# Seven-product matmul of an MLP: pairing whole token blocks instead of token halves

## Chip, cores and metric

The kernel runs on one core of one Trainium2 chip. The metric is the device time of one execution in microseconds (us). The core's engines are TensorE (PE in the rows; PEld is its weight load), VectorE (DVE), ScalarE (ACT), GpSimd (POOL) and SyncE (SP), which issues the DMAs.

## The reference

One layer of a diffusion backbone works on 1152 tokens (1024 latent, 128 context) of 1024 features. Two mixers and their output projection come first; the change touches only the MLP behind them:

```
h   = RMSNorm_pre2(x) * (1 + scale2) + shift2
x   = x + gate2 * RMSNorm_post2(relu(h @ W1)^2 @ W2)     W1 1024 x 4096, W2 4096 x 1024
```

All is fp32. The kernel splits each operand into a high part (rounded to TensorE's fp32r format) and a low part (the rest), and a product is three matmuls: high x high, high x low, low x high.

## The kernel before

**Tokens and tiles.** The normalised tokens lie in SBUF feature-major, in three blocks of 384 tokens (`h2H[b]`, `h2L[b]`, 128 partitions x 8 chunks of 128 features x 384). A scheduler with its own costs (`Sched`) sets the order of all work up to this point; it ends with `Q.run()`, and the two early groups of the first column (L1980) are its last matmuls. From there on the order is the order in which the code is written.

**First product, plain columns.** The hidden features are 32 columns of 128, two to a pair, 16 pairs. The first two pairs (`NPL = 2`, columns m = 0 to 3) are computed plainly in `plain`: for each token block 8 chunks x 3 matmuls of 128x384 (L2050 to L2052), then ScalarE's Relu and Square, and one store of the column to `Fd` in DRAM. `w1_load` fetches a column of W1 (512 KB) into the one tile `raw`; `w1_split` makes w1H on ScalarE (L1718) and w1L on VectorE (L1719). Between the blocks `work` runs: `build` forms the token operands of the seven-product scheme.

**First product, the other 14 pairs.** `strassen` uses the Winograd form of the 2x2 scheme: A is a pair's weights (two columns by two halves of the features), B the tokens (two halves of the features by two halves of the tokens, 576 each, `HT`). Seven products of 4 chunks x 3 matmuls, each on two pieces of 288 columns (L2194), replace eight. A token half is not a block: `h_copies` gathers its parts by DMA into `B11`, and, for want of room, spills `B21` and `B22` to DRAM (`Hd`); they are read back (L2162) when the blocks' own tiles are given up. `T1` to `T4` are sums of these operands, made by `build`.

**Weights of a pair.** `w1_pair` loads both columns (L2102). `w_sums` makes three sums on VectorE (L2126 to L2128), `w_split` the high and low part of one of seven weight words (L2137 on ScalarE, L2138 on VectorE; S4 also needs L2135). They run as hooks between the steps of the pair ahead. Eight pairs also carry 16 small matmuls of the second gate (`late_mm`).

**Evacuation.** Products accumulate in PSUM banks called x, y and z; ScalarE copies x out three times (t1, u2, u4, L2200), VectorE adds them to y or z (L2205), squares (L2180), and the result goes to `Fd` (L2183).

**Second product.** `mlp2` runs 16 groups, each 9 token tiles x 2 halves x 6 matmuls of 128x512 (L2296 to L2298). `g_load` reads back one group's `Fd` and two rows of W2 (L2231, L2234), `g_w` and `g_f` split them (L2240, L2241, L2254, L2255). For the first group these are hooks of the last pair.

Of the kernel before, what the change touches and what calls it, by code (L numbers as in the profile page):

```python
# [10 lines left out]
F32 = mybir.dt.float32  # L11
# [7 lines left out]
D = 1024  # L19
# [183 lines left out]
def hymba_kernel(tc, a, o):  # L203
# [1764 lines left out]
    Q.add("A", ca(1024), lambda: w1_split(0), r=["w1l"], w=["w1s"], take=[w1w], prio=400)  # L1968
    nop("h2k", [("me", j, f) for j in range(6, 10) for f in range(4)])
# [31 lines left out]
    def operand(x, pool):
        HO[x] = [pool.tile([128, 4, HT], F32R, tag=f"o{x}{q}", name=f"o{x}{q}") for q in "HL"]
    for x in ("T1", "T2", "T3", "T4", "B11"):
        operand(x, tb)


    SEG = [((0, 0, 384, 0), (1, 0, 128, 384), (2, 256, 320, 512)), ((1, 128, 384, 0), (2, 0, 256, 256), (2, 320, 384, 512))]

    def h_copies(dst, half, kj, blocks):
        for b, c0, c1, d in SEG[half]:  # L2010
            if b in blocks:
                for q in range(2):
                    SY.dma_start(out=dst[q][:, :, d:d + c1 - c0].bitcast(F32),
                                 in_=(h2H, h2L)[q][b][:, 4 * kj:4 * kj + 4, c0:c1].bitcast(F32))

    def build(k):

        qA = bp.tile([128, 2, HT], F32, tag="q0", name="qA")
        qB = bp.tile([128, 2, HT], F32, tag="q1", name="qB")
        for t, half in ((qA, 0), (qB, 1)):  # L2020
            for b, c0, c1, d in SEG[half]:
                yield lambda t=t, b=b, c0=c0, c1=c1, d=d: V.tensor_tensor(
                    out=t[:, :, d:d + c1 - c0], in0=h2H[b][:, k::4, c0:c1].bitcast(F32), in1=h2L[b][:, k::4, c0:c1].bitcast(F32),
                    op=ALU.add)
# [17 lines left out]
    def plain(m, work):  # L2042

        wH, wL = w1q.pop(m)
        f = bp.tile([128, NT], F32, tag="pf", name="pf")
        f2 = f.rearrange("p (a c) -> p a c", a=2)
        for b in (1, 2, 0):
# [5 lines left out]
            r = bp.tile([128, BLK], F32, tag="r", name="r")  # L2053
            S.activation(out=r, in_=ps, func=AF.Relu)
# [362 lines left out]
```

## Time and profile before

| | |
|---|---|
| median of 3 runs | 1762.05 us (1756.42 to 1762.86) |
| profiled execution, its own time | 1766.09 us |
| its span, first to last instruction | 1764.3 us |
| TensorE busy | 1623.9 us (92%), 13731 matmuls |
| VectorE / ScalarE / GpSimd busy | 64% / 39% / 17% |
| mean granted TensorE clock | 0.968 of full |
| chain that ended last | TensorE 66%, VectorE 13%, DMA 7% |

The busy shares are means over stages with different limits, so the stages are read apart: plain columns to 1011.49 us, first pair to 1047.92, eight pairs with late matmuls to 1236.28, five without to 1347.62, then the second product. A matmul's own duration in the rows (0.29 to 0.40 us) overlaps with its neighbours'; the distance between two starts is what a matmul costs in a stream.

### The profile page before, as it was taken

The page shows a single profiled execution, that of the slowest core. Times are in us where ns is not written, and L with a number is a line of the kernel's source. Part 1 is how long each engine was busy: PE and PEld are TensorE (multiplying, and loading weights), DVE is VectorE, ACT ScalarE, POOL GpSimd, SP SyncE. Part 2 cuts the span into 40 slices and gives each one's busy share as a digit, 9 for nine tenths or more (in the row PEclk, how much of TensorE's full clock was granted, in tenths as well). Part 3 has the DMA queues.
Part 4 walks back from the last instruction along what each step waited for, and adds up shares of the span by engine and source line. Part 5 has one row for each costly group of instructions (what it writes and reads, how often), then busy time and mean ns, then how long its engine had stood idle before and what let it go on. Part 6 is the DMA issues. An engine that isn't in the chain of part 4 may idle for free.

```text
span 1764.3 us, 33783 instructions
## 1 busy us (share of the span) xinstructions
PE 1623.9 (92%) x13731; PEld 1372.9 (78%) x13731; DVE 1134.1 (64%) x1882; ACT 680.9 (39%) x1283; POOL 304.5 (17%) x425
## 2 busy tenths in 40 slices
PE   6799988898899998699996979999999999999996
PEld 2688877788788766566775979999999888888885
DVE  2835675767876878765478644555554566776668
ACT  3734443434325667444346423333334211111112
POOL 3200378858011120211210000000000000000005
PEclk9899999988999999999998989999999999999998
DMA  9545857674564677999554653333335223322413
GB/s 309 193 128 137 218 133 184 163 196 111 133 158 105 152 189 178 206 227 251 169 186 131 186 194 113 108 120 107 102 102 194 100 78 132 106 89 79 148 48 144
DMA packets 322364, 264.95 MB, mean 150 GB/s; under 512 B 105624, under 2 KB 282976, under 8 KB 319648
## 3 DMA queue, kind: packets, MB, share of 16 engines
q1 hardware_dynamic: 320096, 255.23, 50.9%
q0 software_dynamic: 2112, 7.55, 1.3%
q8 instruction: 108, 1.77, 0.4%
q14 instruction: 48, 0.39, 0.1%
HBM read 175.39 MB, written 84.97 MB: 148 GB/s over the span
## 4 chain that ended last, share of the span: by engine, by line
PE 66%; DVE 13%; DMA 7%; POOL 6%; issue 3%; ACT 3%; SPq 2%; DVEq 0%; ACTq 0%; POOLq 0%
PE ps_g L2194 10%; PE ps_G L2194 5%; PE ps_g L531 3%; POOL ar L1028 3%; PE ps_g L532 3%; PE ps_g L533 3%; POOL ar L1024 3%; PE ps_m L2194 3%; PE ps_g L1662 2%; PE ps_m L2297 2%; PE ps_g L2297 2%; PE ps_g L2298 2%; PE ps_m L2298 2%; PE ps_g L2296 2%; PE ps_m L2296 2%
## 5 line engine op out<-in xcount | busy, mean ns | idle before, releaser
L531 PE MATMUL ps_g<-hH,wH 128*128 128x384 f32 x552 | 209.3, 379 | 2.6 <-DVE hH L270 1.9
L532 PE MATMUL ps_g<-hL,wH 128*128 128x384 f32 x552 | 191.6, 347 | 5.5 <-DVE hL L484 5.2
L533 PE MATMUL ps_g<-hH,wL 128*128 128x384 f32 x552 | 190.2, 345 | 0.0
L2281 POOL TENSOR_TENSOR rT<-rT,rT 128x512 f32<-128x512 f32 x8 | 11.8, 1492 | 827.9 <-DVE rT L2279 827.2
L2240 ACT ACTIVATE ws<-w2r 128x1024 fp32r<-128x1024 f32 x32 | 32.3, 1053 | 273.5 <-DVE rB L2302 125.8
L531 PEld LDWEIGHTS ps_g<-hH,wH 128*128 128x128 f32 x552 | 108.1, 196 | 18.0 <-issue 8.5
L532 PEld LDWEIGHTS ps_g<-hL,wH 128*128 128x128 f32 x552 | 108.0, 196 | 9.7 <-DVE hL L484 8.5
L533 PEld LDWEIGHTS ps_g<-hH,wL 128*128 128x128 f32 x552 | 107.6, 195 | 0.0
L1024 POOL TENSOR_TENSOR ar<-ar 128x252 f32<-128x252 f32 (+22 forms) x124 | 82.8, 668 | 41.4 <-DMA ar<-NAd 32.6
L1028 POOL TENSOR_TENSOR ar<-ar 128x252 f32<-128x252 f32 (+22 forms) x124 | 87.3, 704 | 9.3
L1539 DVE TENSOR_TENSOR SV<-ps_m,Dt 64x256 f32<-64x256 f32 x136 | 57.1, 421 | 23.0 <-PE ps_m L1534 16.6
L2200 ACT ACTIVATE tu<-ps_g 128x288 f32<-128x288 f32 x56 | 22.9, 411 | 105.4 <-PE ps_g L2194 93.1
L1503 PE MATMUL ps_G<-SV,r 128*32 128x64 f32 x1152 | 53.7, 226 | 10.1 <-DVE SV L1539 9.5
L1534 PEld LDWEIGHTS ps_m<-SV,IT 128*64 128x64 f32 x1120 | 41.5, 141 | 26.7 <-issue 11.1
L2302 DVE TENSOR_TENSOR rT<-ps_G,rT 128x512 f32<-128x512 f32 x60 | 41.2, 687 | 30.5 <-PE ps_G L2298 30.5
L1534 PE MATMUL ps_m<-SV,IT 128*64 128x64 f32 x1120 | 51.4, 232 | 8.6 <-DVE SV L1539 5.5
L1503 PEld LDWEIGHTS ps_G<-SV,r 128*32 128x32 f32 x1152 | 39.5, 112 | 25.4 <-DVE SV L1539 17.5
L2302 DVE TENSOR_TENSOR rT<-ps_m,rT 128x512 f32<-128x512 f32 x60 | 41.2, 688 | 23.6 <-PE ps_m L2298 23.6
L2302 DVE TENSOR_TENSOR rT<-ps_g,rT 128x512 f32<-128x512 f32 x60 | 41.3, 688 | 22.8 <-PE ps_g L2298 22.8
L2194 PE MATMUL ps_G<-oT4H,ws 128*128 128x288 f32 x224 | 48.2, 301 | 7.4 <-DVE f L2205 7.4
L268 ACT ACTIVATE SV<-ps_G 32x256 f32<-32x256 f32 x95 | 35.7, 375 | 44.9 <-PE ps_G L1519 34.5
L2194 PE MATMUL ps_g<-oT2H,ws 128*128 128x288 f32 x224 | 49.0, 305 | 2.6 <-ACT tu L2200 2.6
(557 smaller groups left out, 4656.2 us busy)
## 6 DMA issues: line engine op xcount, KB each, us to landing
KGd<-ar SPq DMA_DIRECT2D x96, 192.0 KB
r<-KGd SPq DMA_DIRECT2D x36, 512.0 KB
rB<-Fd SPq DMA_DIRECT2D x16, 1152.0 KB
mw<-in_w_mod_dram SPq DMA_DIRECT2D x64, 256.0 KB
w1r<-in_w_mlp_dram SPq DMA_DIRECT2D x32, 512.0 KB
w2r<-in_w_mlp_dram SPq DMA_DIRECT2D x32, 512.0 KB
Fd<-f SPq DMA_DIRECT2D x56, 288.0 KB
raw<-in_w_in_dram SPq DMA_DIRECT2D x26, 512.0 KB
```

The lines of the kernel that those rows point to most:

```text
L531: T.matmul(ps, wH[:, k, :], hH[b][:, k, :], start=(k == 0), stop=False)
L532: T.matmul(ps, wH[:, k, :], hL[b][:, k, :], start=False, stop=False)
L533: T.matmul(ps, wL[:, k, :], hH[b][:, k, :], start=False, stop=(k == 7))
L1024: E.tensor_tensor(out=t, in0=X[:, :, 0:m, j:j + 1].to_broadcast([128, 2, m, w]), in1=n[:, :, j % 8:j % 8 + 1, j + 1:32].to_broadcast([128, ...
L1028: E.tensor_tensor(out=X[:, :, 0:m, j + 1:32], in0=X[:, :, 0:m, j + 1:32], in1=t, op=ALU.subtract)
L1503: T.matmul(RU[n][r0:r0 + 32, 0, p, :], KRG[n][kq][:, e, p, kc, 0:32], SV[n][s % NSV][:, e, p, :], start=True, stop=True)
L1534: T.matmul(x["S"][64 * e:64 * e + 64, p, :], it_()[:, e, p, :], sv_()[:, e, p, :], start=True, stop=True)
L2194: T.matmul(P, wq_, h[:, k, cs[c]], start=(ch not in seen and k == q == 0), stop=(k == 3 and q == 2), skip_group_check=True)
L2296: T.matmul(ps, tok(fH, m), wH[:, hs_], start=(m == 0), stop=False)
L2297: T.matmul(ps, tok(fH, m), wL[:, hs_], start=False, stop=False)
L2298: T.matmul(ps, tok(fL, m), wH[:, hs_], start=False, stop=(m == 1))
L2302: V.tensor_tensor(out=acc_(i)[:, hs_], in0=ps, in1=acc_(i)[:, hs_], op=ALU.add)
```

## The change

The scheme now takes the token blocks as they lie: block 0 is the first half, block 1 the second, 384 tokens each, and block 2 is computed plainly within each pair. Nothing is gathered, spilled or read back. A pair has eleven steps: seven products and four plain ones (E1 and E2 are block 2's two halves of the features), 132 matmuls of 128x384. It uses eight weight words, A21 among them. Results are stored by block, six stores of 192 KB to a pair. The pool `dp` is opened before the plain columns. The weights of column m+1 are split right behind the matmuls of column m's first block, and the load of column 1 is given to the scheduler, behind the split of column 0. The second product finds its tiles in the room of T1 to T4 and of the blocks.

```
+    Q.add("S", 0, lambda: w1_load(1), r=["w1s"], w=["w1l1"], nbytes=524288, prio=400)
...
+    for x, k0, b in (("B11", 0, 0), ("B21", 4, 0), ("B22", 4, 1), ("E1", 0, 2), ("E2", 4, 2)):
+        HO[x] = [h[b][:, k0:k0 + 4, :] for h in (h2H, h2L)]
...
-            for fn in itertools.islice(work, 8):
+            if b == 1 and m + 1 < 2 * NPL:
+                w1_split(m + 1)
+                if m + 2 < 2 * NPL:
+                    w1_load(m + 2)
+                else:
+                    w1_pair(NPL)
+            store(m // 2, m % 2, b, ps)
+            for fn in itertools.islice(work, 4):
                 fn()
...
-            if b == 2:
-                if m + 1 < 2 * NPL:
-                    w1_split(m + 1)
...
+    def store(p, i, b, src, add=None):
+        f = dp.tile([128, BLK], F32, tag="f", name="f", bufs=6)
+        if add is None:
+            S.activation(out=f, in_=src, func=AF.Relu)
+            S.activation(out=f, in_=f, func=AF.Square)
+        else:
+            V.tensor_tensor(out=f, in0=add, in1=src, op=ALU.add)
+            V.scalar_tensor_tensor(out=f, in0=f, scalar=0.0, in1=f, op0=ALU.max, op1=ALU.mult)
+        SY.dma_start(out=Fd[p][:, i, BLK * b:BLK * b + BLK], in_=f)
...
-    ORD0, ORD = (1, 6, 7, 5, 4, 2, 3), (1, 2, 6, 7, 5, 3, 4)
+    STEPS = (("A11", "B11", "x"), ("A11", "E1", "u"), ("A12", "B21", "y"), ("A12", "E2", "u"), ("S2", "T2", "x"), ("S3", "T3", "z"),
+             ("S1", "T1", "x"), ("A21", "E1", "v"), ("A22", "T4", "z"), ("A22", "E2", "v"), ("S4", "B22", "x"))
...
+            if s_ in (0, 4, 6):
+                S.activation(out={0: t1, 4: u2, 6: u4}[s_], in_=ps["x"], func=AF.Copy)
+            if s_ == 2:
+                store(p, 0, 0, ps["y"], t1)
+            if s_ == 3:
+                store(p, 0, 2, ps["u"])
+            if s_ == 6:
+                store(p, 1, 1, ps["z"], u4)
+            if s_ == 8:
+                store(p, 1, 0, ps["z"], u2)
+            if s_ == 9:
+                store(p, 1, 2, ps["v"])
+            if s_ == 10:
+                store(p, 0, 1, ps["x"])
...
-        return {1: [lambda: w_sums(p)], 2: sp_(0), 3: sp_(1, 2), 4: sp_(3), 5: sp_(4, 5), 6: sp_(6)}
+        return {1: [lambda: w_sums(p)], 2: [sp_(0)], 4: [sp_(1)], 5: [sp_(2)], 6: [sp_(3)], 7: [sp_(4)], 8: [sp_(5)], 10: [sp_(6), sp_(7)]}
...
-            hooks = {0: [lambda: g_load(0)], 2: [lambda: g_w(0, 0)], 3: [lambda: g_w(0, 1)], 4: [lambda: g_f(0)]}
+            hooks = {5: [lambda: g_load(0)], 6: [lambda: g_w(0, 0)], 7: [lambda: g_w(0, 1)], 8: [lambda: g_f(0)]}
```

How the instructions stand, at three places. First ScalarE behind the last normalised tokens (h2H), where the plain columns begin; L1718 is the split of column 1's weights, L2029 (now L2016) the high parts of T1 to T4, the rest evacuations. Before:

```order
L268 ACTIVATE h2H_9757<-h_10095 128x384
L2054 ACTIVATE r<-ps_m 128x384
L2058 ACTIVATE pf<-r 128x128
L2059 ACTIVATE pf<-r 128x256
L2054 ACTIVATE r<-ps_P 128x384
L2061 ACTIVATE pf<-r 128x256
L2062 ACTIVATE pf<-r 128x2x64
L2029 ACTIVATE oT1H<-qA 128x576
L2029 ACTIVATE oT2H<-qB 128x576
L2029 ACTIVATE oT3H<-qB 128x576
L2029 ACTIVATE oT4H<-qA 128x576
L1718 ACTIVATE w1H<-w1r 128x1024
```

And of the change at the same place:

```order
L268 ACTIVATE h2H_9757<-h_10097 128x384
L1718 ACTIVATE w1H<-w1r 128x1024
L2090 ACTIVATE f<-ps_m 128x384
L2091 ACTIVATE f<-f 128x384
L2090 ACTIVATE f<-ps_P 128x384
L2091 ACTIVATE f<-f 128x384
L2016 ACTIVATE oT1H<-qA 128x384
L2016 ACTIVATE oT2H<-qB 128x384
```

The split has moved from behind ten instructions to the head.

Second VectorE within a pair, from the first of the three weight sums (L2126, now L2120) on; f is a result, ws a weight word, s the word S4. Before:

```order
L2126 TENSOR_TENSOR sS<-w1r_12341 128x512
L2127 TENSOR_TENSOR sS<-sS,w1r 128x512
L2128 TENSOR_TENSOR w1r_12341<-w1r,w1r_12341 128x512
L2138 TENSOR_TENSOR ws<-w1r,ws 128x512 x2
L2138 TENSOR_TENSOR ws<-sS,ws 128x512
L2205 TENSOR_TENSOR f<-u_12345,ps_G 128x288 x2
L2180 SCALAR_TENSOR_TENSOR f<-f 128x576
L2138 TENSOR_TENSOR ws<-w1r_12341,ws 128x512
```

And of the change:

```order
L2120 TENSOR_TENSOR sS<-w1r_11850 128x512
L2121 TENSOR_TENSOR sS<-sS,w1r 128x512
L2122 TENSOR_TENSOR s_11894<-w1r,w1r_11850 128x512
L2093 TENSOR_TENSOR f<-t_11853,ps_m 128x384
L2094 SCALAR_TENSOR_TENSOR f<-f 128x384
L2132 TENSOR_TENSOR ws<-w1r,ws 128x512 x2
L2075 COPY mw<-ps_s 2x128
```

The sums, which wait for a load, now also stand ahead of the first result (t1 + y); the z sums stay behind them as before.

Third SyncE's queue in the last pair, around the loads of the second product's first group (its f, then two rows of W2, w2r). Before:

```order
L2183 DMA Fd_10117<-f 128x576 x4
L2231 DMA rB_13798<-Fd_10103 128x2304
L2234 DMA w2r<-in_w_mlp_dram 128x1024
L2234 DMA w2r_13801<-in_w_mlp_dram 128x1024
L2183 DMA Fd_10118<-f 128x576 x4
```

And of the change:

```order
L2095 DMA Fd_10119<-f 128x384 x6
L2095 DMA Fd_10120<-f 128x384 x2
L2184 DMA rT2H<-Fd_10105 128x2304
L2187 DMA w2r<-in_w_mlp_dram 128x1024
L2187 DMA w2r_13402<-in_w_mlp_dram 128x1024
L2095 DMA Fd_10120<-f 128x384 x4
```

The load has moved behind the first two results of the last pair, and it goes into the tile of T2.

## Rows read from the trace of the kernel before

**Rows 1.** Stretches: busy us of each engine (instructions), granted clock, DMA share, GB/s

```profile
957.80:1011.49 53.69, 41.99 (x216) 40.85 (x217) 38.46 (x61) 23.44 (x45) 0.00 (x0) 0.87 0.57 170
1011.49:1047.92 36.43, 25.95 (x170) 25.25 (x169) 15.07 (x27) 9.66 (x21) 0.00 (x0) 0.86 0.55 199
1047.92:1236.28 188.36, 188.36 (x1488) 182.37 (x1489) 95.95 (x173) 62.22 (x129) 0.00 (x0) 1.00 0.38 115
1236.28:1347.62 111.34, 111.34 (x843) 111.34 (x842) 58.72 (x98) 40.34 (x81) 0.00 (x0) 1.00 0.35 112
1347.62:1764.30 416.68, 400.48 (x1730) 324.11 (x1728) 281.94 (x399) 87.40 (x135) 23.90 (x16) 0.99 0.31 109
```

**Rows 2.** Waits from 920 to 1060 us: who waited for whom, us, times, longest

```profile
DVE sS L2126 <- DMA w1r<-in_w_mlp_dram: 25.8, 2, 15.4
...
PE ps_G L2194 <- DVE f L2205: 7.4, 1, 7.4
...
PE ps_m L2050 <- ACT w1H L1718: 6.4, 1, 6.4
...
PE ps_g L2050 <- ACT w1H L1718: 2.6, 1, 2.6
...
PE ps_m L2052 <- DVE w1L L1719: 1.8, 1, 1.8
...
PE ps_g L2052 <- DVE w1L L1719: 0.9, 1, 0.9
```

**Rows 3.** TensorE in order of time, plain columns: start us, duration us, instruction

```profile
989.65 0.33 PE L2050 MATMUL ps_g<-h2H,w1H 128*128 128x384 f32 x1
...
1011.32 0.33 PE L2052 MATMUL ps_m<-h2H,w1L 128*128 128x384 f32 x1
```

**Rows 4.** TensorE in order of time, first pair; in brackets the idle time before

```profile
1017.46 0.40 PE L2194 MATMUL ps_g<-oT2H,ws 128*128 128x288 f32 x1 [2.63 <-ACT tu L2200]
...
1019.49 0.45 PE L2194 MATMUL ps_g<-oT2L,ws 128*128 128x288 f32 x1
1019.73 0.69 PE L2194 MATMUL ps_g<-oT2H,ws 128*128 128x288 f32 x2
...
1022.53 0.42 PE L2194 MATMUL ps_G<-oT3H,ws 128*128 128x288 f32 x2
```

**Rows 5.** ScalarE and VectorE in order of time, start of the plain columns

```profile
955.26 0.47 ACT L2054 ACTIVATE r<-ps_m 128x384 f32<-128x384 f32 x1
...
963.10 1.04 ACT L1718 ACTIVATE w1H<-w1r 128x1024 fp32r<-128x1024 f32 x1
...
965.73 1.22 DVE L1719 TENSOR_TENSOR w1L<-w1r,w1H 128x1024 fp32r<-128x1024 f32 x1
```

**Rows 6.** SyncE and VectorE in order of time, last token tile ahead of the MLP

```profile
915.66 0.42 SPq L1825 DMA_DIRECT2D wL<-OBd  x1
...
928.42 0.68 DVE L1913 TENSOR_TENSOR ot<-ps_g,wL 128x512 f32<-128x512 f32 x1
```

**Rows 7.** SyncE and VectorE in order of time, loads of the next pair

```profile
1284.18 1.12 SPq L2102 DMA_DIRECT2D w1r<-in_w_mlp_dram  x2
...
1290.29 0.69 DVE L2126 TENSOR_TENSOR sS<-w1r 128x512 f32<-128x512 f32 x1 [1.59 <-DMA w1r<-in_w_mlp_dram]
...
1106.01 0.69 DVE L2126 TENSOR_TENSOR sS<-w1r 128x512 f32<-128x512 f32 x1 [2.80 <-DMA w1r<-in_w_mlp_dram]
```

**Rows 8.** SyncE and ScalarE in order of time, last pair, first group's loads

```profile
1328.72 0.36 SPq L2231 DMA_DIRECT2D rB<-Fd  x1
...
1338.13 1.06 ACT L2240 ACTIVATE ws<-w2r 128x1024 fp32r<-128x1024 f32 x1 [2.63 <-DMA w2r<-in_w_mlp_dram]
1339.41 1.07 ACT L2240 ACTIVATE ws<-w2r 128x1024 fp32r<-128x1024 f32 x1 [0.21 <-DMA w2r<-in_w_mlp_dram]
```

**Rows 9.** Groups of instructions, 957.8 to 1347.6 us: count, busy us, mean ns

```profile
L2137 ACT ACTIVATE ws<-w1r 128x512 fp32r<-128x512 f32 x56 | 33.5, 621 | 8.8 <-DMA w1r<-in_w_mlp_dram 8.7
...
L2054 ACT ACTIVATE r<-ps_g 128x384 f32<-128x384 f32 x5 | 2.4, 487 | 9.8 <-PE ps_g L2052 9.8
...
L2138 DVE TENSOR_TENSOR ws<-w1r,ws 128x512 fp32r<-128x512 f32 x56 | 37.3, 685 | 3.9 <-ACT ws L2137 3.8
...
L2205 DVE TENSOR_TENSOR f<-u,ps_G 128x288 f32<-128x288 f32 x28 | 12.5, 453 | 36.3 <-ACT u L2200 36.3
```

More of the change, by code (lines that the diff above doesn't have):

```diff
@@ L1985, in hymba_kernel @@
     pWo.close()
-    HT = NT // 2
     NM, NP, NPL = 32, 16, 2
     Fd = [dr.tile([128, 2, NT], F32, name=f"Fd{p}") for p in range(NP)]
-    Hd = {(x, q): dr.tile([128, 4, HT], F32R, name=f"Hd{x}{q}") for x in ("B21", "B22") for q in range(2)}
     pD = ExitStack()
     tb = pool_(pD, "tb", 1)
-    bp = pool_(pD, "bp", 1)
+    dp = pool_(pD, "dp", 1)
     HO = {}
[L2001 to L2014, printed above, removed]
-    def build(k):
[L2018 to L2024, printed above, removed]
+    for x, n in (("T1", BLK), ("T2", 576), ("T3", 576), ("T4", BLK)):
+        HO[x] = [tb.tile([128, 4, n], F32R, tag=f"o{x}{q}", name=f"o{x}{q}")[:, :, 0:BLK] for q in "HL"]
+    for x, k0, b in (("B11", 0, 0), ("B21", 4, 0), ("B22", 4, 1), ("E1", 0, 2), ("E2", 4, 2)):
+        HO[x] = [h[b][:, k0:k0 + 4, :] for h in (h2H, h2L)]
+    def build(k):
+        qA = dp.tile([128, 2, BLK], F32, tag="q0", name="qA")
+        qB = dp.tile([128, 2, BLK], F32, tag="q1", name="qB")
+        for t, b in ((qA, 0), (qB, 1)):
+            yield lambda t=t, b=b: V.tensor_tensor(out=t, in0=h2H[b][:, k::4].bitcast(F32), in1=h2L[b][:, k::4].bitcast(F32), op=ALU.add)
         sub = lambda o_, x, y: lambda: V.tensor_tensor(out=o_, in0=x, in1=y, op=ALU.subtract)
@@ new lines, in strassen @@
+        t1, u2, u4 = [dp.tile([128, BLK], F32, tag=nm, name=nm) for nm in ("t1", "u2", "u4")]
+        for s_, (wx, hx, ch) in enumerate(STEPS):
+            w, h = wop[p, wx], HO[hx]
+            new = ch not in ps
+            if new:
+                ps[ch] = bank(CH[ch], BLK)
+            for k in range(4):
+                for n, (qw, q) in enumerate(((0, 0), (0, 1), (1, 0))):
+                    T.matmul(ps[ch], w[:, qw, k], h[q][:, k, :], start=(new and k == n == 0), stop=(k == 3 and n == 2),
+                             skip_group_check=True)
+            if s_ in (0, 4, 6):
[12 more added lines that the diff above has]
+                store(p, 0, 1, ps["x"])
@@ L2344, in hymba_kernel @@
             for i in range(4):
-                x1_t[i] = room("T4", i // 2, [128, 2, D]) if i % 2 == 0 else x1_t[i - 1]
-            for i in range(4):
-                x1_t[i] = x1_t[i][:, i % 2]
+                x1_t[i] = room(("T1H", "T1L", "T4H", "T4L")[i], [128, D])
                 SY.dma_start(out=x1_t[i], in_=X1d[i][:])
         if g == NP - 1:
-            for i, x in ((4, ("B11", 0)), (6, ("B11", 1)), (8, ("B21", 0))):
-                t = room(*x, [128, 2, D])
+            for i, x in ((4, "T2H"), (6, "T2L"), (8, "T3H")):
+                t = room(x, [128, 2, D])
                 for e in range(2 if i < 8 else 1):
```

143 lines of the change are left out of this document (35 added, 108 removed).

## The prediction, made before the result was known

> **What bounds the kernel now.** I read the table of stretches first, cut at the places where the first MLP product changes its form [rows 1]. From 1047.92 us on TensorE is busy without a break through thirteen pairs and the second product, at full clock. So there only the length of the matmul stream counts, and a faster VectorE or ScalarE brings nothing. The two stretches ahead of it are different: 957.80 to 1011.49 us (three plain columns, m = 1 to 3) has 41.99 us of TensorE work in 53.69 us at a mean clock of 0.87, and the first seven-product pair takes 36.43 us at 0.86. The list of waits then says what TensorE stands for there [rows 2]: in the plain columns for the weights' high part from ScalarE (6.4 + 2.6 us) and their low part from VectorE (1.8 + 0.9 us), in the first pair for a VectorE sum (7.4 us) and a ScalarE copy (2.63 us [rows 4]). Last I read TensorE's rows in order of time for the spacing of matmuls at both clock levels [rows 3, 4], and the three queues around the loads [rows 5 to 8].
>
> **The plain columns.** What is removed here: the operand copies and spills, and the place of the weight split. In the row of ScalarE the split of column 1 starts at 963.10, though the first evacuation after the normalisation starts at 955.26 [rows 5]: evacuations and four operand copies stand between. The change puts the split at the head. ScalarE then has w1H from about 955.4 to 956.4, VectorE needs 1.22 us more [rows 5], so w1L is there at about 957.7. TensorE comes to the column at 957.80 and to its third matmul, the first that reads w1L, two spacings later, at 958.15. That is a cover of 0.45 us; if it is missed, the price is the miss itself. Columns 2 and 3 have over 4 us of cover: ScalarE and VectorE do shorter sums now (384 columns in place of 576), and the loads go out one column earlier. So the three columns cost 216 matmuls at the spacing of 128x384. Between 989.65 and 1011.32 lie 125 of these spacings, 21.67/125 = 0.1734 us each [rows 3]. 216 x 0.1734 = 37.5 us in place of 53.69: **-16.2 us**, of which 11.7 are the four waits and 4.5 the half clock that follows them (the 0.87 of the row).
>
> One transfer moves to an earlier place: SyncE's queue now issues the load of column 1 in front of the last token tile's two loads, and it must first wait for the split of column 0. In the trace the second of these two, wL<-OBd, goes out at 915.66 and is read at 928.42 [rows 6]. It would go out some 3 us later, behind 512 KB; I take that as hidden (about 4 us of cover are left after the transfer) and price it at 0, at most 3.
>
> **The first pair.** Its operands now lie where they were made, so nothing is read back. Its matmuls are 7 products x 4 x 3 = 84 on tokens of blocks 0 and 1 and 2 x 8 x 3 = 48 plain ones on block 2: 132 of 384 columns, 132 x 0.1734 = 22.9 us. The stall of 7.4 us was VectorE, standing up to 15.4 us for the next weights [rows 2], whose load shares the queue with the spilled operands, ahead of the sum that frees the bank. That wait stays in VectorE's order, as the order rows show; only the time of landing changes. The load is issued 5.5 us into the pair (three evacuation steps, six copies of 0.62 us, their subtractions of 0.69 us [rows 9]). A pair's two loads are read 6.1 us after the issue, 1290.29 - 1284.18 [rows 7]; so at 11.6. Then ScalarE, in order, does the copy (0.62), two evacuation steps (0.49 each [rows 9]) and at 13.5 has u2 out of the bank that step 6 writes; TensorE wants step 6 at 6 x 12 x 0.1734 = 12.5. A wait of about 1.1 us is left. 36.43 becomes 24.0: **-12.4 us** (bounds -10 with the clock falling behind that wait, -13.5 without it).
>
> **Thirteen more pairs.** Before, five without the gate's late matmuls take 111.34/5 = 22.27 us, eight with them 188.36/8 = 23.55 [rows 1]. After: 22.9 and 1.28 more. Per pair 36 matmuls fewer, but 384 columns for 288: +0.62 us, x 13 = **+8.1 us**. This is what block 2 costs by being computed plainly. The new evacuations are beside it: ScalarE about 9 us and VectorE about 12 us of the 22.9. Whether they hold TensorE depends on the load. It is issued about 3.3 us into a pair (as now: 1284.18 [rows 7] against a start at 1236.28 + 2 x 22.27 = 1280.82) and read at 9.5. ScalarE's chain (0.62 + 3 x 0.49, with a handover 2.2 us) has u2 out at 11.7 where 12.5 is wanted; VectorE (three sums, two steps of 0.55 each, three subtractions, about 5.4 us) is at z by 15.1, waits for u4 to 15.4 and is done by 16.0 where step 8 is wanted at 16.6. A step of 384 on VectorE is not in the trace; it lies between 0.45 (288) and 0.69 (512) [rows 9]. I take 0 for the waits; they begin where the load lands later than about 10.3.
>
> The Trainium skill speaks against this term. The spacing of 0.1734 us for 384 columns and 0.1325 for 288 are rows [rows 1, 3]. "TensorE: Matmul & The Clock Gate", section "Back-to-back issue gap", gives N/2.4 + 2.5 ns, that is 162.5 and 122.5 ns. By it the wider matmul would cost 0.87 us a pair, not 0.62, and the whole prediction would be 3.5 us later. The trace differs from it at both widths (+11 and +10 ns), and the rows decide; the result would lie inside the forecast's range, so it is no rival.
>
> **Into the second product.** Before, the first group's data are loaded from the last pair's step 0 and TensorE passes over without a gap. Now their room is T2's tile, which is read until step 4 ends, 10.4 us into the pair. The loads were asked for at 1328.72 and ScalarE had the two weight rows at 1338.13 and 1339.41, +9.4 and +10.7 [rows 8]. From 10.6 that is 20.0 and 21.3. Behind them: two copies of 1.06 us, four of 0.68, and on VectorE the low parts (2 x 1.22), one sum and its square, and four subtractions; the first low part of f is done at 25.4, the second row's at 26.7. TensorE is ready at 22.9: it starts its first high parts, then waits about 2.7 us in two pieces. A wait of 2.63 us left the clock at half for some 3.4 us [rows 4], 0.24 in place of 0.13 us, 1.5 us lost. Together **+4.2 us** (0 if the split pieces go ahead of the last pair's leftovers, 7.5 if the loads land 3 us later). The second product itself keeps its 1728 matmuls and its end: 0.
>
> **Sum.** -16.2 - 12.4 + 8.1 + 4.2 = -16.3 us. Against the profiled execution's own 1766.09 us that is 1749.8. That execution lies 4.0 above the median of the runs shown, 1762.05; so the median becomes 1745.8, rounded **1746**.
>
> **Rivals.** (a) *The load decides every pair.* VectorE's sums stand in order ahead of the two z sums, ScalarE's first copy ahead of u2. Each us by which the load lands later than 10.3 is paid in all 13 pairs. For it: six stores of 192 KB in place of four of 288 KB stand on the same queue, and the trace has one pair with the sums at 1106.01 [rows 7], 11.0 after the start at 1047.92 + 2 x 23.55. Against it: of the twelve pairs behind the first ten are read at 8.1 to 9.8, and the bytes are the same. Break-even is 16.3/13 = 1.25 us a pair, a landing at 11.6. In a mild form (11.3) the cost is 13 us, 1759. In the strong form, which decides from 12.2 on and needs the transfer itself to take 3 us longer, it is 2.6 x 13 = 34 us: **1780, slower than before.** (b) *The waits that I add don't come* (ScalarE's step is shorter; f's pieces are taken up one by one): 1.1 + 4.2 us less, 1741. (c) *The weights are split first only in the text:* ScalarE reaches the split late since its head stands for the normalisation, or w1L misses by more than 0.45 us, and the clock falls again. Half of the 16.2 us stays: 1754.
>
> **How the numbers follow.** The forecast 0.60; (b) 0.12; (c) 0.10; (a) mild 0.12, strong 0.06. A measurement of this kernel tells a change apart from none at about 0.5%, 8.8 us, that is below 1753.2. The forecast, (b) and a share of (c) are faster: 0.76. (a) mild and the rest of (c): within, 0.18. (a) strong: slower, 0.06. The range takes in the forecast's bounds, (b), (c) and the runs' own spread: 1738 to 1757; outside lies (a).
>
> **What would show it.** Right: TensorE without a gap from 957.8 to about 995.3 at full clock; pairs of 22.9 and 24.2 us; the second product starting near 1331.5 with VectorE's subtraction as its releaser. Wrong: a wait of column 1 for w1L; waits of T4's or T1's matmuls for VectorE's f or ScalarE's u in every pair (a); a spacing of 384 columns other than 0.173 us in the pairs; or an early change before 957.8, for which I see no reason but the moved load.

## The result, and the profile after

| | before | after |
|---|---|---|
| median, all runs shown | 1762.45 us (1756.42 to 1764.10, 4 runs) | 1738.55 us (1734.32 to 1740.80, 4 runs) |
| profiled execution, its span | 1766.09, 1764.3 us | 1739.05, 1737.3 us |
| TensorE busy, matmuls | 1623.9 us (92%), 13731 | 1621.3 us (93%), 13227 |

The ratio is 0.9868, with an interval of 0.9838 to 0.9898: 23.9 us faster. The prediction had 1746 in a range of 1738 to 1757; the sign is right, and the time lies 0.55 us above the lower end of the range.

The stretches of the trace after, cut at the same events as [rows 1] (three plain columns, first pair, eight pairs with late matmuls, five without, second product). Columns: start and end, length, busy us of PE, PEld, DVE, ACT, POOL with instruction counts, granted clock, DMA share, GB/s:

```profile
953.01:990.45 37.44, 37.44 (x218) 37.44 (x218) 28.84 (x47) 19.37 (x39) 0.00 (x0) 1.00 0.42 129
990.45:1013.44 22.99, 22.99 (x134) 22.85 (x133) 13.24 (x22) 10.89 (x21) 0.00 (x0) 1.00 0.29 89
1013.44:1207.04 193.60, 193.60 (x1202) 186.24 (x1202) 90.50 (x160) 71.38 (x136) 0.00 (x0) 1.00 0.36 112
1207.04:1321.57 114.53, 114.53 (x662) 114.53 (x661) 52.30 (x86) 45.52 (x85) 0.00 (x0) 1.00 0.33 108
1321.57:1737.30 415.73, 399.63 (x1729) 324.50 (x1728) 282.28 (x400) 88.38 (x137) 23.84 (x16) 0.98 0.31 110
```

From 953.01 us to the end of the matmuls TensorE is busy without a break and at full clock: in the first four rows busy time and length are the same number, and the clock is 1.00 where [rows 1] had 0.87 and 0.86. Beside the prediction's terms, in us:

| term | forecast | measured | how |
|---|---|---|---|
| plain columns 1 to 3 | -16.2 | -16.25 | 53.69 to 37.44 |
| first pair | -12.4 | -13.44 | 36.43 to 22.99 |
| thirteen further pairs | +8.1 | +8.43 | 299.70 to 308.13 |
| into and through the second product | +4.2 | -0.95 | 416.68 to 415.73 |
| ahead of the plain columns | 0 | -4.79 | 957.80 to 953.01 |
| sum | -16.3 | -27.0 | spans, 1764.3 to 1737.3 |

The first four terms make -22.2 us. The fifth belongs to a part of the program in which every engine's order stayed as it was (SyncE's got the one moved load); the experiments below show that it differs by more than that from run to run. So about 22.2 us are the change's by one trace of each kernel, and the 23.9 of the medians agree with it.

TensorE's waits from 940 to 1345 us in the trace after (who waited for whom, us in all, times, longest), all of them:

```profile
PE ps_G L469 <- ACT h L475: 2.2, 3, 0.9
PE ps_G L469 <- DVE h L478: 0.7, 1, 0.7
```

L469 is still the normalisation. Of the waits of [rows 2] none is left, and neither of the two that I had added, at the first pair's step 6 and ahead of the second product, came. These two places are therefore what has to be looked at. First the start of column 1, ScalarE, VectorE and TensorE in order of time (start us, duration us, instruction):

```profile
950.62 1.04 ACT L1718 ACTIVATE w1H<-w1r 128x1024 fp32r<-128x1024 f32 x1
951.57 0.47 ACT L2090 ACTIVATE f<-ps_m 128x384 f32<-128x384 f32 x1
...
951.69 1.23 DVE L1719 TENSOR_TENSOR w1L<-w1r,w1H 128x1024 fp32r<-128x1024 f32 x1 [0.39 <-ACT w1H L1718]
...
953.01 0.33 PE L2035 MATMUL ps_m<-h2H,w1H 128*128 128x384 f32 x1
...
953.35 0.33 PE L2037 MATMUL ps_m<-h2H,w1L 128*128 128x384 f32 x1
```

The split has gone from the end of the queue [rows 5] to its head. w1L is done at 952.92 and first read at 953.35: 0.43 us of cover, where I had worked out 0.45. The first pair, load (SyncE), ScalarE, VectorE and TensorE's step 6 (the first matmul on oT1H):

```profile
995.72 1.01 SPq L2084 DMA_DIRECT2D w1r<-in_w_mlp_dram  x2
...
1000.04 0.64 ACT L2131 ACTIVATE ws<-w1r 128x512 fp32r<-128x512 f32 x1 [3.24 <-DMA w1r<-in_w_mlp_dram]
...
1001.51 0.47 ACT L2154 ACTIVATE u<-ps_g 128x384 f32<-128x384 f32 x1
...
1001.69 0.69 DVE L2120 TENSOR_TENSOR sS<-w1r 128x512 f32<-128x512 f32 x1 [4.54 <-DMA w1r<-in_w_mlp_dram]
...
1002.92 0.35 PE L2151 MATMUL ps_g<-oT1H,ws 128*128 128x384 f32 x1
```

The load is asked for 5.3 us into the pair (5.5 in the prediction), and VectorE's first sum (S1, of A21 and A22), which reads the second column, starts 6.0 us after that (6.1 in the prediction). But ScalarE's copy of A11 starts 4.3 us after it: it reads only the first column. I had timed it by the second. So u2 is out at 1001.98, 0.9 us before step 6 and not 1.1 us after. A pair without late matmuls, the same chain (pair's start at 1252.85):

```profile
1255.97 1.01 SPq L2084 DMA_DIRECT2D w1r<-in_w_mlp_dram  x2
...
1260.27 0.63 ACT L2131 ACTIVATE ws<-w1r 128x512 fp32r<-128x512 f32 x1 [3.27 <-DMA w1r<-in_w_mlp_dram]
...
1261.93 0.69 DVE L2120 TENSOR_TENSOR sS<-w1r 128x512 f32<-128x512 f32 x1 [4.59 <-DMA w1r<-in_w_mlp_dram]
...
1268.15 0.55 DVE L2093 TENSOR_TENSOR f<-u,ps_G 128x384 f32<-128x384 f32 x1 [1.34 <-ACT u L2154]
...
1269.51 0.34 PE L2151 MATMUL ps_G<-oT4H,ws 128*128 128x384 f32 x1
```

Here VectorE, in order behind its sums and weight words, has to wait 1.34 us for u4, and z is out at 1268.70, 0.8 us before step 8 writes its bank. So 2.1 us of a later load are covered. Last, the first group's loads in the last pair (start at 1298.66), to be held against [rows 8]:

```profile
1309.25 0.32 SPq L2184 DMA_DIRECT2D rT2H<-Fd  x1
...
1315.65 1.06 ACT L2193 ACTIVATE ws<-w2r 128x1024 fp32r<-128x1024 f32 x1 [1.72 <-DMA w2r<-in_w_mlp_dram]
1316.91 1.06 ACT L2193 ACTIVATE ws<-w2r 128x1024 fp32r<-128x1024 f32 x1 [0.20 <-DMA w2r<-in_w_mlp_dram]
...
1320.21 2.76 DVE L2204 TENSOR_TENSOR rT3H<-rT2H,rT2L 128x576 fp32r<-128x576 f32 x4
...
1321.57 0.39 PE L2245 MATMUL ps_g<-ws,rT2L 128*128 128x512 f32 x1
...
1322.03 0.39 PE L2247 MATMUL ps_g<-ws,rT3H 128*128 128x512 f32 x1
...
1322.73 0.40 PE L2247 MATMUL ps_g<-ws,rT3H 128*128 128x512 f32 x1
```

The issue is 10.6 us into the pair, as forecast. The weight rows are read 6.4 and 7.7 us after it, not 9.4 and 10.7 as before: 3.0 us sooner, and the wait of 2.7 us is gone with them. The low parts of f (rT3H, four pieces) are done at 1320.96, 1321.63, 1322.30 and 1322.97. TensorE's third matmul reads the first piece at 1322.03, 1.1 us later, and its sixth the third piece (the second row's) at 1322.73, 0.4 us later; 0.4 us is therefore the cover of the whole chain.

### The profile page after: what moved, and what is told of

Its sections match the earlier page's. It is cut to its first block, busy times and chain, and to the rows that moved or that the text cites. A ratio compares the mean times of both kernels' runs of the same rounds, so it can differ in the third digit from the quotient of the medians.

```text
span 1737.3 us, 32874 instructions
## 1 busy us (share of the span) xinstructions
PE 1621.3 (93%) x13227; PEld 1373.1 (79%) x13227; DVE 1112.1 (64%) x1838; ACT 694.3 (40%) x1289; POOL 303.5 (17%) x425
## 4 chain that ended last, share of the span: by engine, by line
PE 70%; DVE 13%; DMA 6%; POOL 5%; issue 2%; ACT 2%; SPq 2%; DVEq 0%; POOLq 0%; ACTq 0%
PE ps_g L2151 7%; PE ps_P L2151 7%; PE ps_g L531 4%; PE ps_G L2151 3%; PE ps_g L532 3%; PE ps_g L533 3%; PE ps_g L1662 3%; POOL ar L1028 2%; POOL ar L1024 2%; PE ps_m L2247 2%; PE ps_g L2247 2%; PE ps_m L2246 2%; PE ps_g L2246 2%; PE ps_m L2245 2%; PE ps_g L2245 2%
## 5 line engine op out<-in xcount | busy, mean ns | idle before, releaser
L2151 PE MATMUL ps_P<-h2H,ws 128*128 128x384 f32 x448 | 122.7, 334 | 0.0
L2151 PEld LDWEIGHTS ps_P<-h2H,ws 128*128 128x128 f32 x448 | 81.7, 188 | 0.0
L2151 PE MATMUL ps_P<-h2L,ws 128*128 128x384 f32 x224 | 74.9, 334 | 0.0
L2132 DVE TENSOR_TENSOR ws<-w1r,ws 128x512 fp32r<-128x512 f32 x56 | 37.2, 687 | 53.0 <-ACT ws L2131 53.0
L2251 DVE TENSOR_TENSOR rA<-ps_G,rA 128x512 f32<-128x512 f32 x68 | 46.8, 688 | 36.6 <-PE ps_G L2247 36.6
L2251 DVE TENSOR_TENSOR rA<-ps_m,rA 128x512 f32<-128x512 f32 x67 | 46.2, 689 | 28.4 <-PE ps_m L2247 28.4
L2251 DVE TENSOR_TENSOR rA<-ps_g,rA 128x512 f32<-128x512 f32 x67 | 46.1, 689 | 27.2 <-PE ps_g L2247 27.0
L1534 PEld LDWEIGHTS ps_m<-SV,IT 128*64 128x64 f32 x1120 | 42.0, 143 | 25.9 <-issue 10.6
L2151 PE MATMUL ps_g<-h2H,ws 128*128 128x384 f32 x224 | 59.3, 335 | 0.0
```

The costliest lines, as they stand in the source:

```text
L2151: T.matmul(ps[ch], w[:, qw, k], h[q][:, k, :], start=(new and k == n == 0), stop=(k == 3 and n == 2), skip_group_check=True)
L2251: V.tensor_tensor(out=acc_(i)[:, hs_], in0=ps, in1=acc_(i)[:, hs_], op=ALU.add)
```

## The experiments

### Where TensorE comes to the plain columns

In all twelve kernels TensorE, ScalarE and VectorE have the same order of instructions up to the plain columns. The first matmul of column 0 starts there at (us):

| load of column 1 behind the schedule | load of column 1 within it |
|---|---|
| before 953.38; split first 944.51; split and load first 947.54; load behind 944.88 | after 948.74; split behind 951.19; group load late 947.30; loads swapped 947.89; load 2 us later 942.88; load 4 us later 943.32; traffic back 945.86; stores ahead 946.28 |
| mean 947.6 | mean 946.7 |

One of them undoes just the moved load:

```
-    Q.add("S", 0, lambda: w1_load(1), r=["w1s"], w=["w1l1"], nbytes=524288, prio=400)
...
+    w1_load(1)
     for m in range(2 * NPL):
         plain(m, work)
```

> The changed kernel, with the load of column 1 issued behind the scheduled part in place of within it. The changed kernel's trace comes to the plain columns 4.6 us sooner than before's. Theory: these 4.6 us are differences from run to run of a part in which no order changed, so here that point lies anywhere from 948 to 954 us and does not follow the place of the load; and column 1's weights land in time or not by the place of the load alone: issued at about 945 to 949, landing 5 us later, w1H a little late, a wait of 0 to 4 us at column 1. Rival: the moved load made the early part 4.6 us shorter, and here that point is back at 953.4.

Measured: 1738.38 us in one run, columns 1 to 3 in 37.44 us without a wait, and column 0 starts at 944.88, not at 953.4. The rival falls. The load is asked for at 929.4 here, right behind the last store of the scheduled part on SyncE's queue (the split of column 0 was done at 909.1), and column 1 is split at 946.76 without a wait for it: the wait of 0 to 4 us that I expected was wrong. The table says the rest: the point varies from run to run by 8 to 9 us with either place of the load, and the trace of before happened to be at its upper end. Which event of the first 950 us makes the difference was not tried.

### The place of the split, from both sides

The kernel before with the split alone moved:

```
+            if b == 1 and m + 1 < 2 * NPL:
+                w1_split(m + 1)
             r = bp.tile([128, BLK], F32, tag="r", name="r")
...
-                if m + 1 < 2 * NPL:
-                    w1_split(m + 1)
-                else:
+                if m + 1 == 2 * NPL:
                     w_sums(NPL)
```

> The kernel before, with one part of the change: the weights of column m+1 are split right behind the matmuls of column m's first block; copies, spills, 576-token operands and the order of the loads stay. My theory: the place of the split frees column 1 (its waits for w1H and w1L, 6.4 + 1.8 us, and the half clock behind them go), but the load of column 2 still stands on SyncE's queue behind the store of column 0 and is asked for at about 967, so it is read about 972 while TensorE now comes to column 2 at about 970.3; a wait of 2 to 3.5 us stays there, as large as before. Plain columns 43 to 46 us in place of 53.7; the first pair still waits for VectorE (7 us) because the read-back stays; whole time 8 to 11 us below before. Rival 1: the place of the split alone gives the whole 16.2 us of the plain columns (37.5 us). Rival 2: the split is not what counts, the copies on the queue are: 0 to 3 us.

Measured: ratio to before 0.9989 (0.9970 to 1.0008), no change that can be told, where I had expected 8 to 11 us. Columns 1 to 3 take 48.7 us, 5.0 less, and the pairs 2.0 more (a new wait of 2.8 us for a weight word). SyncE and ScalarE in order of time, and TensorE's waits for w1H:

```profile
958.62 0.63 SPq L1713 DMA_DIRECT2D w1r<-in_w_mlp_dram  x1
...
964.28 1.06 ACT L1718 ACTIVATE w1H<-w1r 128x1024 fp32r<-128x1024 f32 x1 [2.86 <-DMA w1r<-in_w_mlp_dram]
...
982.63 1.06 ACT L1718 ACTIVATE w1H<-w1r 128x1024 fp32r<-128x1024 f32 x1 [5.23 <-DMA w1r<-in_w_mlp_dram]
```

```profile
PE ps_m L2050 <- ACT w1H L1718: 3.1, 1, 3.1
...
PE ps_g L2050 <- ACT w1H L1718: 2.8, 1, 2.8
```

Column 1 no longer waits. Columns 2 and 3 do (3.1 + 2.8 us for w1H, 0.6 each for w1L), since ScalarE now stands for their loads. The mechanism is the one expected, the size isn't: the waits are 7.1 us where I had expected 2 to 3.5, and the mean clock granted in the three columns is 0.93 where after has 1.00. So the load's place was tried too:

```
             if b == 1 and m + 1 < 2 * NPL:
                 w1_split(m + 1)
+                if m + 2 < 2 * NPL:
+                    w1_load(m + 2)
...
-        if m + 1 < 2 * NPL:
-            w1_load(m + 1)
+        if m == 0:
+            w1_load(1)
```

> The kernel before with the weights split first and, other than in the run with the split alone, the loads of columns 2 and 3 asked for right behind that split, ahead of the column's store and the operand copies; copies, spills and 576-token operands stay. With the split alone columns 1 to 3 took 49.7 us: 7.1 us of waits of columns 2 and 3 for weights whose load stood behind a store, and half clock behind them. Theory: place of the split and place of the load together are the whole gain of the plain columns, whatever the operands are: now 37.5 to 40 us, and the first pair still waits 8 us or more for the weights behind the read-back. Whole time 9 to 12 us below the kernel with the split alone. Rival: the copies on the queue still hold the loads, and 4 us or more of waits stay in columns 2 and 3; then the absence of the copies was needed too.

Measured: 1750.81 us, ratio to before 0.9937 (0.9915 to 0.9960), 8.5 us below the split alone by the medians; by the stretches it is only 3.9 us, 5.9 in the columns less 2.0 more in the pairs, and the rest lies in the part ahead that varies from run to run. (The expectation has 49.7 us for the columns with the split alone; the trace has 48.7.) Columns 1 to 3 take 42.8 us, 3 us more than I expected at most. What is left, TensorE's waits from 940 to 1060 us, and the split of column 3:

```profile
PE ps_G L2196 <- DVE f L2207: 8.4, 1, 8.4
PE ps_g L2196 <- DVE ws L2140: 3.2, 1, 3.2
PE ps_m L2052 <- DVE w1L L1719: 3.0, 1, 3.0
...
PE ps_g L2052 <- DVE w1L L1719: 1.1, 1, 1.1
```

```profile
978.08 1.04 ACT L1718 ACTIVATE w1H<-w1r 128x1024 fp32r<-128x1024 f32 x1
...
981.92 1.22 DVE L1719 TENSOR_TENSOR w1L<-w1r,w1H 128x1024 fp32r<-128x1024 f32 x1
```

w1H is in time, and now w1L is late: the high part of column 3 is there at 979.1, but VectorE comes to it at 981.92, behind the operand sums of 576 tokens (two rows of 1.5 us just ahead). So neither pure theory held. Taken in this order, the gain of 16.2 us has three parts: 5.0 by the split's place, 5.9 by the load's, and 5.4 left over. The left-over part I put down to VectorE's and ScalarE's shorter lists, which is what 384-token operands without pieces bring; the waits for w1L behind the sums speak for it, but no run shortened the lists alone. The first pair's 8.4 us stay, as expected: its load still follows the read-back.

From the other side, the changed kernel with the split and the load behind it put back behind block 2:

```
-            if b == 1 and m + 1 < 2 * NPL:
-                w1_split(m + 1)
...
             store(m // 2, m % 2, b, ps)
             for fn in itertools.islice(work, 4):
                 fn()
+            if b == 2 and m + 1 < 2 * NPL:
+                w1_split(m + 1)
...
```

> The changed kernel with one part undone: the weights of the next column (and the load behind them) stand behind the evacuation of block 2 again. My theory: ScalarE then reaches the split of column 1 behind four evacuation steps and two high parts that wait for VectorE, at about 957, where TensorE wants the column at 953; TensorE waits 5 us for w1H and 1.2 for w1L and the clock falls for some 3.5 us: plain columns 37.5 + 6.2 + 1 to 2 = 45 to 46 us, columns 2 and 3 without a wait. Whole time 7 to 9 us above the changed kernel, still below before. Rival 1: all of the 16 us come back (53 us), if columns 2 and 3 wait too. Rival 2: nothing comes back, the shorter evacuations cover it.

Measured: 1742.3 us, ratio to before 0.9898 (0.9866 to 0.9930), against 0.9868 with the split first. TensorE in order of time at columns 1 and 3:

```profile
958.59 0.44 PE L2035 MATMUL ps_m<-h2H,w1H 128*128 128x384 f32 x1 [1.95 <-ACT w1H L1718]
958.86 0.34 PE L2036 MATMUL ps_m<-h2L,w1H 128*128 128x384 f32 x1
959.84 0.44 PE L2037 MATMUL ps_m<-h2H,w1L 128*128 128x384 f32 x1 [0.64 <-DVE w1L L1719]
...
988.13 0.44 PE L2037 MATMUL ps_m<-h2H,w1L 128*128 128x384 f32 x1 [1.10 <-DVE w1L L1719]
```

The waits of column 1 came where expected, but shorter, 1.95 and 0.64 us for 5 and 1.2: ScalarE reaches the split 6.3 us after column 0's first matmul (957.49 against 951.19) where I had worked out 8.3, and TensorE was ready 1.0 us late at 956.46, since column 0 ran partly at half clock here. Columns 1 to 3 take 43.9 us from there, 6.5 more than after, a little under the 45 to 46 us expected; but 1.1 us of it is a wait at column 3, where I had expected none. By the medians the whole time is 3.8 us above the changed kernel, not 7 to 9. Both rivals (nothing, and all 16 us) fall.

From this side the places of the split and the load behind it are worth 6.5 us together, from the other side 10.9 (5.0 and 5.9). The parts are not independent: with the rest of the change in place a late split costs less. So none of them has a share of its own of the 16.2 us.

### The queue behind the first pair's wait

Bytes of the read-back put into the queue again:

```
+    for i in range(4):
+        SY.dma_start(out=Zd[i].rearrange("p a c -> p (a c)"), in_=zs[i // 2][:, 2304 * (i % 2):2304 * (i % 2) + 2304])
     w1_pair(NPL + 1)
```

> The changed kernel with the bytes of the spilled operands' read-back put into the queue again: four DRAM to DRAM copies of 1.18 MB ahead of the second pair's weight load; nothing uses them. Theory: the wait of 7.4 us in the first pair was the load standing behind this traffic. The load is read some 10 to 15 us later than the 6.0 us after its issue, and the first pair is 5 to 12 us longer than its 22.9, with VectorE's f as the releaser and the clock at half behind it; the pairs behind it are as they were. Rival: the wait came from VectorE's longer sums and pieces, not from the queue: under 2 us.

Measured: 1751.54 us in one run; the first pair takes 38.1 us in place of 22.99, every other pair is unchanged (24.20 and 22.90). SyncE, ScalarE's copy and TensorE in order of time:

```profile
992.85 9.05 SPq L2084 DMA_DIRECT2D w1r<-in_w_mlp_dram  x2
...
1010.57 0.63 ACT L2131 ACTIVATE ws<-w1r 128x512 fp32r<-128x512 f32 x1 [16.65 <-DMA w1r<-in_w_mlp_dram]
...
1012.56 0.69 PE L2151 MATMUL ps_g<-oT1H,ws 128*128 128x384 f32 x1 [12.36 <-ACT u L2154]
```

The rival as the only cause (VectorE's longer sums) falls: with the short sums of the change the traffic alone gives 15.1 us. Whether the longer sums had a share in the kernel before was not tried, and the copies, DRAM to DRAM, are like the read-back (DRAM to SBUF) in bytes, not in kind. The load came as late as expected (the copy starts 17.7 us after the issue); the pair is longer than the 5 to 12 us expected, since TensorE stands 12.4 us and then runs at half clock (granted 0.50 from 1012.56 to 1018.1). The releaser is u, not f: in this order ScalarE's copy stands ahead of u2, and the waited-for step comes first. It is the chain that the prediction priced at 1.1 us, with a copy 13.4 us later than in after.

### How late a pair's load may come

The rival of the prediction that ended on the slow side, with its threshold. A small load into the same tile goes ahead, which the real one must wait for; once, and twice one behind the other:

```
     def w1_pair(p):
...
+        for _ in range(1 if p > NPL + 1 else 0):
+            SY.dma_start(out=w1r[p][0][:, 0:1], in_=w1v[:, 0:1, 256 * p:256 * p + 128])
```

> The changed kernel with a small load (64 KB) into the same tile ahead of each of twelve pairs' weight loads; the real load must wait for it and so comes about 2 us later. Theory: in a pair without late matmuls the first column is read 7.6 us after the start and the sums 9.25; the cover is 2.3 us at u2 (step 6) and 2.1 at z (step 8), so with 2 us more no pair waits, or the four pairs without late matmuls wait up to 0.5 us each: 0 to 2 us in all. Rival: a late load is paid from the first us on (no cover), 12 x 2 = 24 us.

> As the run before, with two small loads one behind the other, so the weights come about 4 us later. Theory: the cover of 2.1 us is used up; four pairs without late matmuls wait 1.9 us each and eight with them (1.28 us more cover) 0.6 each, 12 us, and up to 1.5 us more wherever the wait lets the clock fall: 12 to 25 us above the changed kernel, so about as slow as before or a little faster; releasers VectorE's f at step 8 or ScalarE's u at step 6. Rival: no cover, 12 x 4 = 48 us, slower than before. Other rival: VectorE and ScalarE catch up within the pair, under 5 us.

Measured, once: 1733.73 us in one run, no wait of TensorE listed in any pair, and the first product's pairs take 331.4 us, as in after (331.1). Twice: 1754.26 us, ratio to before 0.9962 (0.9946 to 0.9979), and the pairs take 347.8 us, 16.7 more. TensorE's waits there:

```profile
PE ps_G L2153 <- DVE f L2095: 7.4, 11, 1.8
PE ps_g L2153 <- ACT u L2156: 2.6, 6, 0.7
```

Both halves came as expected (0 to 2, and 12 to 25 us), with both releasers. The pairs are now 11.7 us slower than those of before, and of the 23.9 us only 7.7 are left by the medians. So the cover is real, over 1.9 us (the small load delays the real one's issue by about that much) and under 3.8 (two of them), and past it a load is paid in every pair. The run with one small load shows the edge: in the four pairs without late matmuls VectorE's sums start 10.88, 11.03, 11.18 and 11.29 us into the pair, and the pairs take 22.91, 22.91, 22.93 and 23.04 us. For such a pair the threshold is thus a landing of about 11.1 us, 2.0 us behind the 9.1 of after, as the rows of after had said. The rival was a sound one; it just needs a load more than 2 us later than the queue brings it.

### The order of a pair's two loads

```
-        for i in range(2):
+        for i in (1, 0):
             SY.dma_start(out=w1r[p][i], in_=w1v[:, :, 128 * (2 * p + i):128 * (2 * p + i) + 128])
```

> The changed kernel with the two loads of each pair's weights in the other order: column 2 of the pair first. ScalarE's first copy (A11) then reads the tile that lands second. Theory: my forecast of a wait of 1.1 us at step 6 of the first pair rested on a copy that I timed by the later of the two loads (6.0 us after the issue), while it reads only the first (4.3 us). With the order turned round the copy stands 1.7 us later; in the first pair u2 is then out 0.7 us after TensorE wants step 6, a wait of 0.5 to 1 us there; the other pairs had 1.3 us and more of cover and show no wait or one below 0.4 us. Whole time +0.5 to +3 us. Rival: u2 is not what decides, no wait in the first pair.

Measured: 1739.17 us in one run, no wait in any pair. A pair without late matmuls, to be held against the one of after (start at 1252.98):

```profile
1255.50 1.01 SPq L2084 DMA_DIRECT2D w1r<-in_w_mlp_dram  x2
...
1259.63 0.69 DVE L2120 TENSOR_TENSOR sS<-w1r 128x512 f32<-128x512 f32 x1 [2.17 <-DMA w1r<-in_w_mlp_dram]
...
1261.42 0.63 ACT L2131 ACTIVATE ws<-w1r 128x512 fp32r<-128x512 f32 x1 [4.30 <-DMA w1r<-in_w_mlp_dram]
```

Here the sum starts 4.1 us after the first issue and the copy 5.9; in after it was 6.0 and 4.3. The two have changed places with their loads, which shows that each reads its own column alone: the copy waits for the first, the sum for the second. Whether that decides the wait at the first pair's step 6 the run leaves open. There the tile of the second column comes free earlier, so that load went out 3 us sooner (992.69), and ScalarE's copy stood 9.4 us after the pair's start, as in after (9.6): the edit did not delay what it was meant to delay. Over all pairs ScalarE waited 56.2 us for its loads in place of 43.1, 1.0 us a pair, and TensorE felt nothing of it.

### Into the second product

Two runs make the first group's loads later: by two steps of the pair, and by two stores ahead of them.

```
-            hooks = {5: [lambda: g_load(0)], 6: [lambda: g_w(0, 0)], 7: [lambda: g_w(0, 1)], 8: [lambda: g_f(0)]}
+            hooks = {7: [lambda: g_load(0)], 8: [lambda: g_w(0, 0)], 9: [lambda: g_w(0, 1)], 10: [lambda: g_f(0)]}
```

> The changed kernel with the loads and splits of the second product's first group two steps (4.16 us) later in the last pair. Theory: the loads land 6.4 and 7.7 us after their issue also here, since the queue is quiet there; in the changed kernel the first low part of f was ready some 0.6 us before TensorE wanted it, so 4.16 - 0.6 = 3.6 us of wait appear at the start of the second product, in one or two pieces, releaser VectorE's subtraction, and the clock falls for about 1.5 us more: 4 to 5.5 us in all. Rival: f's pieces are taken up one at a time and TensorE has enough started groups to fill the gap: under 1.5 us.

Measured: 1747.03 us in one run. TensorE stands 5.2 us, and the second product is 3.9 us longer. ScalarE and TensorE in order of time:

```profile
1321.14 1.06 ACT L2193 ACTIVATE ws<-w2r 128x1024 fp32r<-128x1024 f32 x1 [8.51 <-DMA w2r<-in_w_mlp_dram]
...
1325.64 0.79 PE L2245 MATMUL ps_g<-ws,rT2L 128*128 128x512 f32 x1 [5.21 <-ACT rT2L L2203]
1326.23 0.63 PE L2246 MATMUL ps_g<-ws,rT2L 128*128 128x512 f32 x1
1326.66 0.63 PE L2247 MATMUL ps_g<-ws,rT3H 128*128 128x512 f32 x1
```

The wait came, with more than the 4 to 5.5 us expected: 5.4 us in the last pair and 2.0 by half clock at the start of the second product, where the first ten spacings are 0.43 us for 0.23 (until about 1329.6). The other 1.9 us by which the second product is longer can't be put on the load: its further spacings add up to 398.77 us for 396.90 in after, and they do the same in the run with the load of column 1 behind the schedule, where TensorE does not wait; the cause is open. The load was moved past one more store on SyncE's queue, and that store waits for VectorE's f of step 6: the issue is 6.3 us later, not 4.16. The weights were read 6.9 us after the issue (6.4 expected), and ScalarE put four evacuation steps between its splits; so the releaser is ScalarE's high part of f (rT2L) and not VectorE's subtraction.

```
+        if g == 0:
+            Zd = [dr.tile([128, 2, 288], F32, name=f"Zd{i}") for i in range(2)]
+            for z in Zd:
+                SY.dma_start(out=z[:], in_=h2H[0][:, 0:2, 0:288].bitcast(F32))
         SY.dma_start(out=fr, in_=Fd[g][:])
```

> The changed kernel with two stores of 288 KB (token data to DRAM, used by nothing) directly ahead of the load of the second product's first group. In the kernel before, two stores of that size shared the time of that load, and the weight rows were read 9.4 and 10.7 us after the issue; in the changed kernel there were none and it was 6.4 and 7.7. Theory: it was the bytes, not the place: now 8 to 9.5 and 9.3 to 10.8 us, the issue is the same or up to 1 us later, and TensorE starts the second product 1 to 3 us late or waits that long within its first ten matmuls, 1 to 4.5 us in all with the clock, the wait that I had forecast. Rival: the first two loads land as before (under 7.2 us), TensorE does not wait.

Measured: 1739.84 us in one run. ScalarE in order of time, and TensorE's waits from 1300 to 1400 us:

```profile
1316.23 1.06 ACT L2197 ACTIVATE ws<-w2r 128x1024 fp32r<-128x1024 f32 x1 [3.39 <-DMA w2r<-in_w_mlp_dram]
1317.61 1.06 ACT L2197 ACTIVATE ws<-w2r 128x1024 fp32r<-128x1024 f32 x1 [0.32 <-DMA w2r<-in_w_mlp_dram]
```

```profile
PE ps_g L2251 <- DVE rT3H L2208: 1.0, 2, 0.6
```

Issued at 1308.87, the rows are read 7.4 and 8.7 us after it; that is between theory (8 us and more) and rival (under 7.2). The issue is 0.7 us later in the pair, so the rows stand 1.7 us later than in after. TensorE waits 1.0 us in two pieces for VectorE's low parts, and the second product takes 1.9 us more (1.5 of it in TensorE's spacings). With the 0.4 us of cover of the second row's low part, 1.7 us give 1.3, between the two: so the chain that I had worked out is right, piece for piece. The bytes of two stores explain at most 1.0 of the 3.0 us by which the load was slower before, since without them the first row is read 6.3 to 6.8 us after the issue in seven traces of the change's order. The other 2.0 stay open. The stores did not stand as before, either: there one went out 0.4 us ahead of the load and one 4.5 us behind it (1328.29 and 1333.25, load 1328.72), here both ahead; and the changed kernel is not without any, one of 192 KB goes out 1.0 us ahead (1308.26).

## Why the prediction was right, and where its sum was off

**Plain columns, -16.2: right, -16.25.** 216 spacings of 0.1734 us, at full clock, with the cover of w1L within 0.02 us of the one worked out. But the reason given was too narrow. I put it on the split's place at the head of ScalarE's queue; the runs show that this alone is worth 5.0 us of the 16.2, and that the rest needs the earlier loads and, as far as the waits show, the shorter sums, which I had named only as cover of columns 2 and 3. (That cover is 3.4 and 7.7 us in the trace after; I had said over 4.) Rival (c) did not come: the cover of w1L is 0.41 us or more in all eight traces that have the change's order there, and none of them waits.

**Moved load, 0: right.** No wait, and no effect on the part ahead that could be told from the run's own spread.

**First pair, -12.4: -13.4.** The issue (5.3 us, forecast 5.5) and the sums (6.0, forecast 6.1) were right. The step that failed is "then ScalarE, in order, does the copy": I let it start when the second column had landed, and it needs only the first, as the run with the two loads in the other order shows. That is 1.7 us, and the wait of 1.1 us became a cover of 0.9. (From the copy's start to u2 it is 1.94 us, which fits the 13.5 of the prediction; the steps listed there add up to 13.2.)

**Thirteen pairs, +8.1: +8.4.** Pairs of 22.90 and 24.20 us, forecast 22.9 and 24.2; most of the 0.3 is rounding. A step of 384 on VectorE takes 0.55 us, as taken. That rows and not the rule decide the matmul's cost held: a pair of 132 matmuls at 22.90 us is 0.1735 us each. The Trainium skill's "TensorE: Matmul & The Clock Gate", section "Back-to-back issue gap", gives 0.1625 by its formula, and the trace does not agree with it. But the Trainium skill states this formula there for a single matmul, and says of 512 columns that a stream takes less; the prediction used it as a rule for streams. Here the stream takes more. Rival (a) lay 2 us away, as the two delayed loads show; I had put its threshold at a landing of 10.3 us, and it is about 11.1.

**Into the second product, +4.2: -0.95.** This is the step with the largest error. The chain behind the load was right, the load's own time was not: I took 9.4 and 10.7 us from [rows 8], and gave no bound for a load that lands sooner. It was 6.4 and 7.7. With a load 3.0 us later and the cover of 0.4 the rows of after give, as an estimate, 2.6 us of wait against my 2.7. Why the load was slower before is shown for at most 1.0 of the 3.0 us. The -0.95 that came in its place is mostly TensorE's spacing: the 1727 spacings of the second product add up to 399.23 us in after and 400.09 in before. That difference repeats (400.09 in three traces with before's order, 399.23 in six with the change's), but one trace without any wait there, the one with the load behind the schedule, has 401.28; what sets it was not tried.

**The sum.** So rival (b), 1741, is what happened as far as the number goes: neither wait that I had added came. But they stayed away for another reason than (b) gave (a shorter step of ScalarE, f's pieces taken up one by one): each time the data that the first instruction needs were there sooner. I gave it 0.12, though both waits rested on a load's time, and each had 0 among its own bounds. The range held with 0.55 us to spare, because it took in (b) and the runs' own spread. The four measured terms, -22.2 us, put against the median of before give 1740; 1738.55 was measured. The early change ahead of 957.8 us, for which I saw no reason but the moved load, does not follow that load, and no run shows another reason of the change's: it is of the size of the spread between runs, and a profiled execution 4 us above the median should have been a hint where to look for it.

## What to carry to other kernels

When a wait sits at the head of a chain through two in-order engines and a queue, moving one of the three only shows the next: here the split's place alone gave 5.0 of 16.2 us, and the rest came only with the load behind it and, it seems, the shorter list of the other engine. Time an instruction by the transfer that it reads, not by the last of its group, and a load by rows in which the same other traffic runs. A move on an issuing queue is priced by what it is moved past: two steps made the issue 6.3 us later and not 4.2, because a store ahead of it had to wait.

## What the runs showed of the hardware that was not expected

The first 950 us of the same instruction order end anywhere from 942.9 to 953.4 us in twelve traces, while the thirteen further pairs repeat to 0.01 us (24.20, or 22.91 without late matmuls, wherever none waits). And a wait does not always cost clock: the waits of 1.95 and 0.64 us ahead of column 1 (split behind) were followed by ten spacings of 0.32 us (granted clock 0.51 from 960.2 to 963.6), while one of 2.99 us for w1L (split and load first) was followed by spacings of 0.17 to 0.18 at once (granted clock 1.00 from 976 to 989). So the half clock behind a wait, which I had counted as 1.5 us in the sum of the second product's term, is a term with 0 as its lower bound.
